# Three modulation edits at the start of a two-layer diffusion trunk: two blocks loaded first, blocks in pairs, two on VectorE

## The chip, the core and the metric

The kernel runs on one core of a Trainium2 chip. The metric is the device time of one execution in microseconds (us). Names of engines: PE is TensorE's matrix engine (PEld its weight loads), DVE is VectorE, ACT is ScalarE, POOL is GpSimd, and SP (SyncE) is the queue from which nearly all loads are issued.

## The reference

A trunk of two layers over 512 latent tokens and 256 context tokens, model width 2048, all in float32. What matters here is the start of a layer: a modulation vector is computed from the conditioning, and the normalized input is scaled and shifted by it before the input projection.

```python
shift, scale, gate = jnp.split(jax.nn.silu(c) @ ada_w + ada_b, 3, axis=-1)
shift_c, scale_c, gate_c = jnp.split(jax.nn.silu(c_ctx) @ ada_w + ada_b, 3, axis=-1)
h = rms_norm(x, norm_w) * (1.0 + scale[:, None]) + shift[:, None]
hc = rms_norm(xc, norm_w) * (1.0 + scale_c) + shift_c
(a_u, a_v, a_z, b_q, ...) = split_columns(h @ w_in)
...
y = jnp.concatenate([y_a, y_b, y_c], axis=-1) @ w_out
x_new = x + gate[:, None] * y
```

`ada_w` is 2048 x 6144 for each layer (50 MB). Behind the projection stand three branches (a gated MLP, a recurrent scan, differential attention) and an output projection; the change does not touch them.

## The kernel before, in words

The input lies transposed in memory: 16 tiles of 128 channels (`kt` 0 to 15) by 768 tokens. The columns of `ada_w` are cut into 24 blocks of 256 for each layer, 2 MB each: blocks 0 to 7 give the shift, 8 to 15 the scale (with the factor `gmul`), 16 to 23 the gate. Block b of the shift and block 8 + b of the scale together serve the tiles kt = 2b and 2b + 1.

A block is computed in one of two ways. `ada_pe` fetches it in five tiles of 128 x 768 and one of 128 x 256 (16 slices of the 2048 rows, three to a tile), multiplies each slice on PE with the conditioning (`sc`, 32 columns wide), copies the sum out of PSUM on VectorE (L271), folds it with two small matmuls against `sel` (in the pack of small constants) and ends in `ada_finish` (L221 adds the bias, L226 makes `gmul`). The tiles are taken in turn from 12 buffers (`ada_slot`): four named K and eight named adaw, which later hold the activations of kt 12 to 15; for the last blocks K, A and B. `ada_dve` fetches a block in eight tiles of 128 x 512 (two slices each, two buffers named adas) and multiplies and adds each slice on VectorE, two instructions a slice (L286 for the first, L288 for the rest), then transposes and reduces (L294, L296); `ada_close` folds it on PE. It is a generator that yields after each slice, so that other code can move it on by steps. In the kernel before, `ada_dve` is used for blocks 16 to 23 of layer 0 and all of layer 1, as a filler behind the lead stage.

Layer 0 begins so: the 16 tiles of x are loaded, ScalarE squares them and VectorE adds the squares up (L161); `rstd_broadcast` turns the sum into a factor for each token and spreads it over the partitions (`WT`). Then comes the lead stage in `run_layer`: four projections (`pp` and `a` in PSUM) run side by side over kt. For each kt, `h_tile` makes the modulated tile as a high part (`hi`, ScalarE L325) and a low part (`lo`, VectorE L326) of a product (`T`, VectorE L322), and PE adds three products (hi x wh, lo x wh, hi x wl) to each of the four projections, in pieces of 512 and 256 tokens. The weights come in groups of four kt: four tiles of 256 KB (`raw`), each split into `wh` (L332) and `wl` (L333). Ahead of each kt, `pre(kt + AHEAD)` with `AHEAD = 2` issues one modulation block, shift and scale by turns. After kt 15 the token groups (`TokGroup`) begin.

Who goes first: loads stay in program order on the SP queue, at most eight under way; a load that has to wait for its buffer holds up all loads behind it. On the other engines a scheduler orders the instructions when the program is built, and each engine then works through its own list strictly in order.

Of the kernel before, what the change touches and what calls it, by code (L numbers as in the profile page):

```python
# [11 lines left out]
F32 = mybir.dt.float32  # L12
# [9 lines left out]
P = 128  # L22
D = 2048
KT = D // P
# [19 lines left out]
def view(t, offset, dims):  # L44
    return bass.AP(t.tensor, t.offset + offset, [list(t.ap[0])] + [list(d) for d in dims])
# [3 lines left out]
def trunk(  # L49
# [10 lines left out]
    gp = ctx.enter_context(tc.tile_pool(name="gp", bufs=1))  # L60
# [23 lines left out]
    def load(dst, src):  # L84
        i = nc.sync.dma_start(dst, src)
        if pinned[0]:
            tc.keep_in_program_order(i)


    def nm(s):  # L90
        uid[0] += 1
        return f"{s}_{uid[0]}"

    BUFS = dict(A6=2, B6=2, C6=2, K3=4, Q3=4, T3=4, WT=2)
# [4 lines left out]
    def g3(tag, dt=F32, shape=(P, T)):  # L99
        return gp.tile(list(shape), dt, tag=tag, bufs=BUFS[tag], name=nm(tag))  # L100

    def small(tag, shape, dt=F32, bufs=3):
        return sp.tile(list(shape), dt, tag=tag, bufs=bufs, name=nm(tag))
# [4 lines left out]
    def p_one(shape):  # L108
        return ps.tile(list(shape), F32, tag="a1", bufs=4, name=nm("a1"))
# [38 lines left out]
    def xslot(i):  # L148
        if 8 <= i < 12:
            return g3("Q3")  # L150
        if i % 2 == 0:
            xslots.append(g6("A6" if i < 4 else "B6" if i < 8 else "C6"))
        return xslots[-1][:, i % 2, :]

    def square_into(acc, src, a, b, first, eng):
        if first:
            S.activation(acc[:, a:b], src[:, a:b], AF.Square)
            return
        sq = g3("T3")
        S.activation(sq[:, a:b], src[:, a:b], AF.Square)  # L160
        eng.tensor_tensor(acc[:, a:b], acc[:, a:b], sq[:, a:b], op=ALU.add)  # L161
# [58 lines left out]
    def ada_finish(l, n0, nn, pt):  # L220
        V.tensor_tensor(  # L221
            adaT[l][:, n0 : n0 + nn, :], pt, view(adab_s[l], n0, [[1, nn], [0, 2]]), op=ALU.add
        )
        if KT <= n0 < 2 * KT:
            k0 = n0 - KT
            V.scalar_tensor_tensor(  # L226
                gmul[l][:, k0 : k0 + nn, :],
                adaT[l][:, n0 : n0 + nn, :],
                1.0,
                view(normw_s[l], k0, [[1, nn], [0, 2]]),  # L230
                op0=ALU.add,
                op1=ALU.mult,
            )

    def ada_src(l, nb, kt, n):
        return ada_w[l, nb, :, kt : kt + n, :]
# [3 lines left out]
    def ada_slot(n0):  # L240
        tags = ["K3"] * 4
        if n0 < 12:
            tags = tags + [f"{w}{i}" for i in range(12, 16) for w in ("hi", "lo")]
        else:
            tags = tags + ["A6", "A6", "B6", "B6"]
        slots[0] += 1
        tag = tags[slots[0] % len(tags)]
        if tag in BUFS:
            return g3(tag, shape=(P, 3, 256))
        return ap.tile([P, 3, 256], F32, tag=tag, bufs=1, name=nm("adaw"))  # L250

    def ada_pe(l, n0):
        pa = p_one([P, 260])
        kt = 0
        while kt < KT:
            nk = min(3, KT - kt)
            wt = ada_slot(n0 % KT)
            load(wt[:, :nk, :], ada_src(l, n0 // 2, kt, nk))
            for k in range(nk):
                j = (kt + k) % 4  # L260
                PE.matmul(
                    pa[32 * j : 32 * j + 32, :256],
                    sc[:, kt + k, :],
                    wt[:, k, :],
                    start=(kt + k < 4),
                    stop=(kt + k >= KT - 4),
                    tile_position=(0, 32 * j),
                )
            kt += nk
        sb = g3("T3", shape=(P, 256))  # L270
        V.tensor_copy(sb, pa[:, :256])  # L271
        pt = pa[:, 256:260].rearrange("p (n i) -> p n i", i=2)
        for n in range(2):
            PE.matmul(pt[:, n, :], sb[:, n * P : (n + 1) * P], sel_s, start=True, stop=True)
        ada_finish(l, n0, 2, pt)

    def ada_dve(l, nb):
        acc = gp.tile([P, 2, 256], F32, tag="acc", bufs=1, name=nm("acc"))
        for kt in range(KT):
            if kt % 2 == 0:  # L280
                wt = wp.tile([P, 2, 256], F32, tag="adas", bufs=2, name=nm("adas"))
                load(wt, ada_src(l, nb, kt, 2))
            for i in range(2):
                sca = cc_s[:, kt, i : i + 1]
                if kt == 0:
                    V.tensor_scalar(acc[:, i, :], wt[:, 0, :], sca, None, op0=ALU.mult)  # L286
                else:
                    V.scalar_tensor_tensor(  # L288
                        acc[:, i, :], wt[:, kt % 2, :], sca, acc[:, i, :], op0=ALU.mult, op1=ALU.add
                    )  # L290
            yield

        tr = g3("T3", shape=(P, 16, 32))
        V.transpose(tr.rearrange("p a b -> p (a b)"), acc.rearrange("p a b -> p (a b)"))  # L294
        red = small("red", [P, T // 32], bufs=2)
        V.tensor_reduce(red[:, :16], tr, axis=AX.X, op=ALU.add)  # L296
        return red

    def ada_close(l, nb, red):
        pt = p_one([P, 2, 2])  # L300
        for q in range(4):
            PE.matmul(
                pt[32 * q : 32 * q + 32, :, :],
                fold,
                view(red, q, [[4, 2], [8, 2]]),
                start=True,
                stop=True,
                tile_position=(0, 32 * q),
            )
        ada_finish(l, 2 * nb, 2, pt)  # L310
# [111 lines left out]
    def prepare():  # L422
        nonlocal mask_s
        mask_s = const("mask", [P, MASKS * 32], U8)
        V.tensor_copy(mask_s, parts["masks"])
# [500 lines left out]
    AHEAD = 2  # L926
# [7 lines left out]
    TOKLAST = 4  # L934
    TOKFILL = (2, 2, 2, 3)
    LEVEL = 4
    LATE = 6
    TAILK = 2
    PREP = 16
# [2 lines left out]
    def advance(fill, n):  # L942
        for _ in range(n):
            if next(fill, 0) == 0:
                break

    def run_layer(l, xs, rb, pre, fillers, chain=None, ahead=()):
# [62 lines left out]
        for i in range(4):  # L1010
            pt = TokGroup(NCH if i < 3 else L.nch)
            for _ in pt.mm(nxt, acts):
                at += 1
                if at % LEVEL == 0:
                    next(lv, None)
# [95 lines left out]
        else:  # L1111
            for m in last:
                load(xscr[m], xs2[m])
            return xs2, rb, chain, ahead

    load(pk, pack)
    xs = []
    acc = g3("WT")
    for kt in range(KT):
        x = xslot(kt)  # L1120
        load(x, xT[kt])
        square_into(acc, x, 0, T, kt == 0, V)
        xs.append(x)
    def pre0(i):
        if i < KT:
            ada_pe(0, KT * (i % 2) + i - i % 2)
        if i == PREP:
            prepare()

    pre0(0)  # L1130
    rb = g3("WT")
    for _ in rstd_broadcast(acc, rb, 0, T):
        pass
    for i in range(1, AHEAD):
        pre0(i)

    def fill():
        late = None
        for l, b0 in ((0, 16), (1, 0)):
            for b in range(b0, 24):  # L1140
                steps = ada_dve(l, b)
                for _ in range(LATE):
                    next(steps)
                    yield
                if late is not None:
                    ada_close(*late)
                late = (l, b, (yield from steps))
        ada_close(*late)

    xs, rb, chain, ahead = run_layer(0, xs, rb, pre0, fill())  # L1150
    run_layer(1, xs, rb, lambda g: None, iter(()), chain, ahead)

# [85 lines left out]
```

## Time and profile before

| what | value |
|---|---|
| three timed runs, us | 2852.78, 2847.98, 2848.84 (median 2848.84) |
| profiled execution, us | 2852.29 |
| its span, us | 2850.2 |
| PE busy over the span | 2754.7 us, 97% |
| DVE, ACT, POOL busy | 55%, 34%, 11% |
| granted TensorE clock, mean | 0.99 of full speed |
| lead stage (first lead matmul to first token matmul) | 45.64 to 166.46 us |

The profiled execution is one run; its own time is its span and some 2 us around it. Busy time of an engine says nothing by itself: what counts is which wait ends last in the stage that is changed.

### The profile page before, as it was taken

The numbers are of one execution on the slowest core, as the hardware profiler recorded it, in microseconds if no ns is written. First come the engines' busy times: TensorE is split into PE (matmuls) and PEld (weight loads), VectorE is DVE, ScalarE is ACT, GpSimd is POOL, SyncE is SP. The second block draws the span as 40 slices with busy tenths as digits, with TensorE's granted clock in tenths as the row PEclk, the third lists the DMA queues.
The fourth block names the chain that finished last, engine by engine and source line by source line (L and its number), as shares of the span: only waits on it lengthen the run. The fifth ranks groups of instructions, "written<-read, shape, count | busy, mean of one in ns | idle before, by whom it ended". The sixth has DMA issues, their size and how long they took to land.

```text
span 2850.2 us, 44886 instructions
## 1 busy us (share of the span) xinstructions
PE 2754.7 (97%) x17524; PEld 2335.7 (82%) x17524; DVE 1566.4 (55%) x3224; ACT 966.2 (34%) x1852; POOL 324.1 (11%) x307
## 2 busy tenths in 40 slices
PE   5998999999999999999999999999999999999997
PEld 3676788888888888888888878888888888888786
DVE  4448867467687776766574272122444555554534
ACT  3222212323344434432311242223333544554321
POOL 0011000332000000001011011000342000000222
PEclk9999999999999999999999999999999999999998
DMA  9825555334343333435553222223232232234533
GB/s 347 276 93 175 177 158 158 85 104 133 95 119 101 108 105 98 122 93 171 177 146 105 80 77 87 89 89 96 75 86 73 74 85 60 82 93 125 166 97 94
DMA packets 184499, 340.24 MB, mean 119 GB/s; under 512 B 19296, under 2 KB 37856, under 8 KB 184288
## 3 DMA queue, kind: packets, MB, share of 16 engines
q1 hardware_dynamic: 177664, 325.33, 38.6%
q10 hardware_dynamic: 6624, 12.06, 1.1%
q8 instruction: 137, 2.24, 0.3%
q14 instruction: 74, 0.61, 0.1%
HBM read 306.91 MB, written 30.41 MB: 118 GB/s over the span
## 4 chain that ended last, share of the span: by engine, by line
PE 84%; DMA 6%; DVE 5%; issue 3%; POOL 1%; ACT 1%; SPq 0%; DVEq 0%; POOLq 0%; ACTq 0%
PE pp L78 68%; PE a L78 14%; DMA adas<-in_ada_w_dram 3%; DVE acc L288 2%; PE a L82 2%; DVE wl L333 1%; DMA adaw<-in_ada_w_dram 1%; POOL A L618 1%; POOL A L620 0%; DMA T<-y 0%; DMA raw<-in_w_in_dram 0%; DMA A<-in_ada_w_dram 0%; DMA B<-in_xT_dram 0%; DMA C<-in_xT_dram 0%; DVE C L616 0%
## 5 line engine op out<-in xcount | busy, mean ns | idle before, releaser
L78 PE MATMUL pp<-hi,wh 128*128 128x512 f32 (+1 forms) x3248 | 1134.3, 351 | 11.0 <-ACT hi L332 4.8
L78 PE MATMUL pp<-lo,wh 128*128 128x512 f32 (+1 forms) x3248 | 1136.6, 350 | 1.6 <-DVE lo L326 1.1
L78 PE MATMUL pp<-hi,wl 128*128 128x512 f32 (+1 forms) x3248 | 1130.9, 349 | 0.0
L333 DVE TENSOR_TENSOR wl<-raw,wh 128x512 fp32r<-128x512 f32 x634 | 448.3, 709 | 659.5 <-ACT wh L332 623.9
L332 ACT CAST wh<-raw 128x512 fp32r<-128x512 f32 x634 | 392.6, 621 | 1189.1 <-PE pp L78 1004.9
L78 PEld LDWEIGHTS pp<-hi,wh 128*128 128x128 f32 x3248 | 614.4, 190 | 94.6 <-ACT hi L332 5.3
L78 PEld LDWEIGHTS pp<-lo,wh 128*128 128x128 f32 x3248 | 616.1, 190 | 85.1 <-issue 6.7
L78 PEld LDWEIGHTS pp<-hi,wl 128*128 128x128 f32 x3248 | 615.0, 189 | 76.1 <-issue 0.2
L288 DVE SCALAR_TENSOR_TENSOR acc<-adas,cc_s,acc 128x256 f32<-128x256 f32 x960 | 421.5, 490 | 89.2 <-DMA adas<-in_ada_w_dram 87.8
L78 PE MATMUL pp<-wh,hi 128*128 128x512 f32 x512 | 200.7, 392 | 0.8 <-DVE WT L501 0.8
L78 PE MATMUL pp<-wl,hi 128*128 128x512 f32 x512 | 199.8, 390 | 0.0
L78 PE MATMUL pp<-wh,lo 128*128 128x512 f32 x512 | 199.5, 390 | 0.0
L830 POOL TENSOR_TENSOR ars<-e,mhalf 128x1 f32<-128x1 f32 x40 | 25.2, 630 | 962.8 <-DVE e L828 962.8
L78 PEld LDWEIGHTS pp<-wh,hi 128*128 128x128 f32 x512 | 96.5, 189 | 21.4 <-issue 1.2
L78 PEld LDWEIGHTS pp<-wh,lo 128*128 128x128 f32 x512 | 96.4, 188 | 20.3
L78 PEld LDWEIGHTS pp<-wl,hi 128*128 128x128 f32 x512 | 96.6, 189 | 19.9
L78 PE MATMUL a<-K,Q 128*128 128x512 f32 (+2 forms) x592 | 108.0, 321 | 0.9 <-DVE adaT L221 0.8
L793 ACT ACTIVATE C<-a,nb 128x256 f32<-128x256 f32 (+1 forms) x144 | 80.6, 567 | 57.5 <-DVE nb L789 54.7
L78 PEld LDWEIGHTS a<-K,Q 128*128 128x128 f32 x592 | 87.7, 190 | 10.5 <-DVE adaT L221 1.3
L78 PE MATMUL a<-wh,hi 128*128 128x512 f32 x224 | 90.7, 405 | 0.0
L78 PE MATMUL a<-wl,hi 128*128 128x512 f32 x224 | 88.3, 394 | 1.5 <-DVE wl L333 1.5
L78 PE MATMUL a<-wh,lo 128*128 128x512 f32 x224 | 88.3, 394 | 0.0
(220 smaller groups left out, 2526.2 us busy)
## 6 DMA issues: line engine op xcount, KB each, us to landing
raw<-in_w_in_dram SPq DMA_DIRECT2D x384, 256.0 KB, 3.1
adas<-in_ada_w_dram SPq DMA_DIRECT2D x256, 256.0 KB, 2.9
raw<-in_w_tok_dram SPq DMA_DIRECT2D x128, 256.0 KB, 2.7
raw<-in_w_out_dram SPq DMA_DIRECT2D x128, 256.0 KB, 3.1
adaw<-in_ada_w_dram SPq DMA_DIRECT2D x42, 384.0 KB, 7.2
t<-T ACTq DMA_DIRECT2D x46, 256.0 KB, 2.6
K<-in_ada_w_dram SPq DMA_DIRECT2D x28, 384.0 KB, 7.3
A<-t SPq DMA_DIRECT2D x11, 768.0 KB, 5.2
```

The costliest lines, as they stand in the source:

```text
L78: return PE.kept(nc.tensor.matmul(*args, **kw))
L82: return PE.kept(nc.tensor.transpose(*args, **kw))
L288: V.scalar_tensor_tensor(acc[:, i, :], wt[:, kt % 2, :], sca, acc[:, i, :], op0=ALU.mult, op1=ALU.add)
L332: S.copy(hi, src)
L333: V.tensor_tensor(lo, src, hi.bitcast(F32), op=ALU.subtract)
L618: G.tensor_tensor(kf, kf, view(tot, stride + 1, [[2, J], [0, m]]), op=ALU.mult)
L793: S.activation(pr[:, m, lo:hi], pt[:, : hi - lo], AF.Exp, bias=nb, scale=SCALE, accum_out=sums[:, m, i : i + 1] if len(parts) == 2 else sm ...
L830: G.tensor_tensor(rs, e0, mhalf[:, 0:1], op=ALU.pow)
```

## The change

Three edits, all in layer 0's start. `first_ada(0)` and `first_ada(1)` (block 0 for the shift and block 8 for the scale) stand ahead of the loads of x. In `pre0`, blocks are issued in pairs at every second kt instead of one at each kt. Blocks 7 and 15, which serve kt 14 and 15, are no longer computed by PE: `side_ada` computes them one after the other with `ada_dve`, moved on by `SIDE = 3` slices at each kt; its running sum takes one of the four buffers named T.

```diff
-    def ada_dve(l, nb):
-        acc = gp.tile([P, 2, 256], F32, tag="acc", bufs=1, name=nm("acc"))
+    def ada_dve(l, nb, tag="acc"):
+        acc = g3(tag, shape=(P, 2, 256)) if tag in BUFS else gp.tile([P, 2, 256], F32, tag=tag, bufs=1, name=nm(tag))
...
+    SIDE = 3
...
+    def first_ada(i):
+        ada_pe(0, KT * (i % 2) + i - i % 2)
+
+    def side_ada():
+        for nb in (KT // 2 - 1, KT - 1):
+            red = yield from ada_dve(0, nb, "T3")
+            ada_close(0, nb, red)
+
     load(pk, pack)
+    first_ada(0)
+    first_ada(1)
     xs = []
     acc = g3("WT")
     for kt in range(KT):
...
+    side = side_ada()
+
     def pre0(i):
-        if i < KT:
-            ada_pe(0, KT * (i % 2) + i - i % 2)
+        if i % 2 == 0 and i < KT - 2:
+            first_ada(i)
+            first_ada(i + 1)
+        if i < KT - 2:
+            advance(side, SIDE)
+        else:
+            advance(side, 1000)
         if i == PREP:
             prepare()
 
-    pre0(0)
     rb = g3("WT")
     for _ in rstd_broadcast(acc, rb, 0, T):
         pass
-    for i in range(1, AHEAD):
-        pre0(i)
```

The load queue (SP) behind the first group of weight tiles, before: the two constant tables `rope`, and then the tiles of the next blocks, one after the other.

```order
L85 DMA raw_334<-in_w_in_dram 128x512
L85 DMA rope_c<-in_rope_dram 128x512
L85 DMA rope_s<-in_rope_dram 128x512
L85 DMA K_70_341<-in_ada_w_dram 128x768
L85 DMA K_71_346<-in_ada_w_dram 128x768
L85 DMA K_72_351<-in_ada_w_dram 128x768
```

The same queue of the changed kernel, from the last tile of the pair for kt 2 and 3 to the first tiles of the pair for kt 4 and 5.

```order
L85 DMA K_83_400<-in_ada_w_dram 128x256
L85 DMA adas_410<-in_ada_w_dram 128x512
L85 DMA adas_416<-in_ada_w_dram 128x512
L85 DMA rope_c<-in_rope_dram 128x512
L85 DMA rope_s<-in_rope_dram 128x512
L85 DMA adas_455<-in_ada_w_dram 128x512
L85 DMA K_96_495<-in_ada_w_dram 128x768
L85 DMA K_97_500<-in_ada_w_dram 128x768
```

Three tiles of a side block now stand between one pair and the next. The third, adas_455, takes the buffer of adas_410, and the pair's tiles stand behind it.

VectorE's list from the copy of a finished block to the low part of kt 2, before (a_91 is a block's sum in PSUM).

```order
L271 COPY T_98_504<-a_91_475 128x256
L226 SCALAR_TENSOR_TENSOR gmul_96<-adaT_94,pack 128x4
L322 SCALAR_TENSOR_TENSOR T_101_511<-A_5_156,gmul_96,WT_255 128x512
L322 SCALAR_TENSOR_TENSOR T_101_511<-A_5_156,gmul_96,WT_255 128x256
L326 SCALAR_TENSOR_TENSOR lo_100_510<-T_101_511,adaT_94,hi_99_509 128x512
```

The same place in the changed kernel (a_95 and a_103 are the pair of blocks for kt 4 and 5, which the list has ahead of kt 2).

```order
L271 COPY T_102_523<-a_95_494 128x256
L288 SCALAR_TENSOR_TENSOR T_85_409<-adas_563,cc_s,T_85_409 128x256 x4
L221 TENSOR_TENSOR adaT_94<-a_95_494,pack 128x4
L271 COPY T_110_557<-a_103_528 128x256
L322 SCALAR_TENSOR_TENSOR T_115_575<-A_21_225,gmul_96,WT_290 128x512
L322 SCALAR_TENSOR_TENSOR T_115_575<-A_21_225,gmul_96,WT_290 128x256
L322 SCALAR_TENSOR_TENSOR T_119_616<-A_21_225,gmul_96,WT_290 128x512
L288 SCALAR_TENSOR_TENSOR T_85_409<-adas_569,cc_s,T_85_409 128x256
L322 SCALAR_TENSOR_TENSOR T_119_616<-A_21_225,gmul_96,WT_290 128x256
L288 SCALAR_TENSOR_TENSOR T_85_409<-adas_569,cc_s,T_85_409 128x256
L221 TENSOR_TENSOR adaT_94<-a_103_528,pack 128x4
L326 SCALAR_TENSOR_TENSOR lo_114_574<-T_115_575,adaT_94,hi_113_573 128x512
```

The products of kt 2 and 3 now stand behind both copies of the pair and behind four adds of a side tile, and the low part of kt 2 behind those of kt 3.

PE's list at kt 1, before: parts of a block (sc) stand between the lead projections.

```order
L78 MATMUL a_56_315<-hi_88_442,wl_337 128x512
L78 MATMUL a_102_542<-adaw_543,sc 32x256 x3
L78 MATMUL pp_312<-lo_89_443,wh_318 128x256
L78 MATMUL pp_312<-hi_88_442,wl_319 128x256
L78 MATMUL pp_313<-lo_89_443,wh_324 128x256
```

In the changed kernel the last projections of kt 1 are followed by the whole pair, tile after tile.

```order
L78 MATMUL pp_313<-hi_92_461,wh_336 128x256
L78 MATMUL pp_313<-lo_93_462,wh_336 128x256
L78 MATMUL pp_313<-hi_92_461,wl_337 128x256
L78 MATMUL a_95_494<-K_96_495,sc 32x256 x3
L78 MATMUL a_95_494<-K_97_500,sc 32x256 x3
L78 MATMUL a_95_494<-K_98_505,sc 32x256 x3
L78 MATMUL a_95_494<-adaw_510,sc 32x256 x3
```

No projection matmul stands between the tiles of a pair any more; those of kt 2 follow when the pair is through.

## Rows read from the trace of the kernel before

**Rows 1.** The page's first line.

```profile
span 2850.2 us, 44886 instructions
```

**Rows 2.** Windows: start:end, length, busy us by engine, PEclk, DMA share, GB/s.

```profile
45.60:166.00 120.40, 115.23 (x849) 78.88 (x850) 52.84 (x113) 28.77 (x52) 0.00 (x0) 0.99 0.75 255
...
76.00:84.00 8.00, 8.00 (x64) 4.75 (x64) 6.16 (x13) 3.29 (x7) 0.00 (x0) 1.00 1.03 403
...
148.00:152.00 4.00, 2.68 (x17) 1.89 (x16) 2.46 (x7) 1.12 (x2) 0.00 (x0) 1.00 0.24 70
152.00:156.00 4.00, 3.44 (x12) 2.48 (x10) 4.00 (x9) 2.24 (x4) 0.00 (x0) 0.68 0.00 0
```

**Rows 3.** PE's timeline: start, duration; kt 0, kt 10, first token matmul.

```profile
45.64 0.74 PE L78 MATMUL pp<-hi,wh 128*128 128x512 f32 x2 [0.81 <-ACT hi L325]
...
125.88 0.73 PE L78 MATMUL pp<-hi,wh 128*128 128x512 f32 x2
...
166.46 0.40 PE L78 MATMUL a<-wh,hi 128*128 128x512 f32 x1
```

**Rows 4.** PE's timeline: neighbouring projection matmuls of 512 and 256 columns.

```profile
159.69 0.39 PE L78 MATMUL pp<-lo,wh 128*128 128x512 f32 x1
...
160.15 0.28 PE L78 MATMUL pp<-hi,wh 128*128 128x256 f32 x1
...
160.74 0.28 PE L78 MATMUL pp<-hi,wl 128*128 128x256 f32 x1
```

**Rows 5.** The chain that ended last, 45 to 170 us.

```profile
67.08 3.45 PE a L78 x50
...
125.77 8.17 DMA A<-in_ada_w_dram
```

**Rows 6.** ScalarE's timeline: first and fourth weight tile of the first group.

```profile
32.65 0.62 ACT L332 CAST wh<-raw 128x512 fp32r<-128x512 f32 x1 [10.30 <-DMA raw<-in_w_in_dram]
...
36.49 0.62 ACT L332 CAST wh<-raw 128x512 fp32r<-128x512 f32 x1 [0.21 <-DMA raw<-in_w_in_dram]
```

**Rows 7.** Timeline: weight loads of PE that waited for modulation tiles.

```profile
24.40 0.19 PEld L78 LDWEIGHTS a<-K,sc 128*32 128x32 f32 x6 [0.78 <-DMA K<-in_ada_w_dram]
...
26.39 0.52 PEld L78 LDWEIGHTS a<-adaw,sc 128*32 128x32 f32 x8 [0.80 <-DMA adaw<-in_ada_w_dram]
```

**Rows 8.** The tile adas, 190 to 640 us: ns min/median/max; landing in us.

```profile
L288 DVE SCALAR_TENSOR_TENSOR acc<-adas,cc_s,acc x421: 435/479/1901, 198.5 to 639.7; 128x256 f32<-128x256 f32 x141
L85 SPq DMA_DIRECT2D adas<-in_ada_w_dram x114: 327/328/436, 194.8 to 599.4; - x114
L286 DVE TENSOR_SCALAR acc<-adas,cc_s x30: 336/345/928, 197.9 to 638.8; 128x256 f32<-128x256 f32 x30
...
DMA to landing us min/median/max: 2.5/2.9/5.0
```

**Rows 9.** Timeline, 14 to 46 us: from the squares' sum to kt 0.

```profile
14.00 10.52 DVE L161 TENSOR_TENSOR WT<-WT,T 128x768 f32<-128x768 f32 x10
...
27.93 0.97 DVE L171 STREAM_TRANSPOSE T<-WT 128x768 f32<-128x768 f32 x1
...
28.93 0.95 DVE L173 TENSOR_REDUCE red<-T 128x24 f32<-128x768 f32 x1
...
33.30 0.69 DVE L333 TENSOR_TENSOR wl<-raw,wh 128x512 fp32r<-128x512 f32 x1 [0.40 <-ACT wh L332]
...
37.01 0.37 ACT L201 COPY WT<-a 128x256 f32<-128x256 f32 x1
...
43.75 0.42 DVE L271 COPY T<-a 128x256 f32<-128x256 f32 x1 [1.38 <-PE a L78]
44.09 1.14 DVE L322 SCALAR_TENSOR_TENSOR T<-A,gmul,WT 128x512 f32<-128x512 f32 x2
...
44.87 1.12 ACT L325 ACTIVATE hi<-T,adaT 128x512 fp32r<-128x512 f32 x2 [7.49 <-DVE T L322]
...
45.62 1.15 DVE L326 SCALAR_TENSOR_TENSOR lo<-T,adaT,hi 128x512 fp32r<-128x512 f32 x2 [0.32 <-ACT hi L325]
```

**Rows 10.** The load queue's waits, 60 to 165 us: for what, us, times, longest.

```profile
SPq L85 <- PE a L78: 36.2, 26, 5.2
```

## The prediction

> **What bounds the kernel now.** The profiled execution spans 2850.2 us [rows 1] and took 2852.29 us; the three timed runs have a median of 2848.84, so what I work out on the span is carried over as a difference and set on the median. Over the whole span the matrix engine is busy 97%, so the first thing to read is where it is not: I went from the page's slices to the windows of the beginning, because all edits lie there.
>
> I call the lead stage the time from the first lead matmul (45.64 us) to the first matmul of the token group (166.46) [rows 3]. In it PE is busy 115 of 120 us and the DMA engines three quarters of the time [rows 2]. The reader should see that both are nearly full, in a stage where each of the 16 input tiles (kt 0 to 15) needs 4.2 us of projection matmuls and one 2 MB modulation block. The 4.2 comes from the spacing of neighbours, 0.23 us for 512 columns (159.69 to 160.15, halved) and 0.118 for 256 (160.15 to 160.74, over five) [rows 4], times 12 of each. A block's 16 matmuls cost about 2.2 us when its tiles have landed: 50 records in 3.45 us, two records to a matmul [rows 5]. The start of kt 0 is at 45.64 and that of kt 10 at 125.88 [rows 3]: 80.2 us for five pairs of tiles, 16.05 a pair; the last six tiles and their last blocks take 40.6.
>
> The loads are all on one queue in program order. Its longest waits in this stage are for PE, 36.2 us in 26 waits [rows 10]: a modulation tile can be fetched only when PE has emptied an older one of the 12 buffers. While transfers flow they move at 403 GB/s [rows 2], and two tiles of 384 KB land 0.99 us apart (26.39 minus 24.40, halved) [rows 7]. A pair of blocks is 10 such tiles and two thirds of one: **10.6 us**. The four 256 KB weight tiles of a group land slower, 1.28 us each (36.49 minus 32.65, over three) [rows 6]: **5.1 us** a group.
>
> **The change, part by part.**
>
> *Blocks 0 and 8 ahead of the input.* The queue up to the first weight tile carries the same bytes in another order, so that tile still lands at about 32.6 and the fourth at 36.4 [rows 6]. The input's last tile lands some 10.6 us later than before. The squares' sums ended at 24.5; they now start about 9 us later and end near 33. Then three weight splits (0.69 each) stand among the transposition and the reduction (0.97 and 0.95), which end near 37.3. From there to the broadcast factor it took 7.5 us before (29.88 to 37.38) [rows 9], so 44.8. Two blocks of PE work now lie in a time when PE has nothing else.
>
> *Pairs, and the end of the interleaving.* The next pair's tiles follow the weight tiles and land by 36.4 + 10.6 = 47.0, later than the broadcast. In the new PE order the pair stands as one burst ahead of the projection matmuls, and in VectorE's order kt 0's multiply stands behind the copies of both blocks. So kt 0 starts after the burst (47.3), a copy (0.42), two multiplies of the side block (0.34 each, 0.7), the tile's multiply (0.78 to ScalarE's start) and ScalarE's add (0.77 to PE's start) [rows 3, 8, 9]: **50.0**, 4.4 us later than before.
>
> *The side blocks (7 and 15) on VectorE.* Their 64 instructions are cheap: 0.48 us each [rows 8], 31 us, and VectorE is busy 53 of the stage's 120 [rows 2]. Their loads are not. There are two side buffers. In each round the third side tile has to wait until VectorE has done with the round's first one, and the last of those reads stands behind the burst, in most rounds behind the copies that follow it. The queue is in order, so all 12 tiles of the next pair (and every other round the four weight tiles) stand behind that third tile. Before, the queue ran ahead as buffers came free; now it stands still once a pair, from the landing of the second side tile until VectorE has come round. A side tile that meets an empty queue landed 2.9 us after issue (2.5 to 5.0) [rows 8].
>
> So from the issue I of a third side tile to the end of the next burst it takes 2.9 + 10.6 + 0.3 (the last matmul) = 13.8 us, or 18.9 where weights come between. From the burst to the next I I follow VectorE's new order with the durations of [rows 8, 9]: a side tile lands 0.4 after the burst (two thirds of 0.99 behind the pair's last tile), 0.48 a side instruction, 0.42 a copy, 1.14 a tile's multiply, 1.15 a tile's low part.
> - First round: burst 47.3; copy, two side multiplies, two tile multiplies (2.28), two side adds: I = 51.9.
> - Burst 65.7; four side adds stand ahead of the second copy: I = 68.0; kt 2 starts at 70.0.
> - Burst 86.9 (weights); two adds, copy, one tile, two adds: I = 90.8.
> - Burst 104.6; two adds, copy, two tiles, two adds: I = 109.6.
> - Burst 128.5 (weights); copy, two tiles, two adds, the low parts with two more adds: I = 135.7.
> - Burst 149.5; four adds, a weight split (0.69), a transposition (0.65, two thirds of the 0.97), multiply and add: kt 10 starts at **154.7**.
>
> PE's own work on a pair (8.4 us, some 2 more until the low part is there) ends before the next tiles have landed (60 against 65 in the first round), so it costs nothing there; without that cover it would.
>
> *The end.* The last six tiles have no block among them: 6 x 4.2 = 25.1, and 2.5 us in which kt 10's first four matmuls are done and VectorE has three more tiles ahead of the low part. The stage ends at 182.3 against 166.46: **15.8 us later**. Per part: +4.4 for kt 0, five pairs at 20.9 instead of 16.05 (+24.5), and 27.6 instead of 40.6 for the rest (-13.0). What comes behind is the same in order but for a few swaps, and waits for this stage; I cost it at nothing. On the median: 2848.8 + 15.8 = 2864.6, **2865**.
>
> **Bounds of the terms.** Landing on an empty queue 2.5 to 5.0: -2 to +10.5 in five rounds. I take 2.9, the median of 114 such loads. Weight tiles at the big tiles' rate (0.67 each) instead of 1.28: -4.9 in two rounds. The new order's waits on VectorE read wrong by half a microsecond: 2.5 either way. So this case holds +8 to +28, 2857 to 2877.
>
> For the same load the page "DMA: Bandwidth & Descriptors" of the Trainium skill (Anatomy of one DMA) gives about 2.0 us fixed plus the bytes at 436 GB/s, by my estimate 2.6 for 256 KB; the sum would be 1.5 us less, and the row decides.
>
> After 148 to 152 us, in which PE worked 2.7 of 4, the granted clock was 0.68 in the next 4 us [rows 2], partly the lower level of 1.2 GHz: 1.3 us lost. Each new pair starts after such a gap. Five of six starts lie under the wait for tiles; the last does not, so this adds at most 1.3, inside the range. The page "TensorE: Matmul & The Clock Gate" of the Trainium skill (HAM oscillation) says that waiting for DMA between bursts sends the engine back to half speed each time; it speaks against the change, and by it alone six starts would cost 8.
>
> **The rivals.**
> - *The loads do not stand still* (faster). If the third side tile found its buffer free, a round would last as long as its bytes: 10.6 + 3 x 0.66 + half of 5.1, 15.1. kt 10 at 125.6, the stage's end at 153: -13, 2836. For it: the queue's 36 us of waits for PE [rows 10] are what pairs and an early start could remove. Against it: the reader of the first tile stands behind the burst, and PE's own round is longer than 15.1 (next rival). It decides where the mean round falls under 17.8 us ((166.46 - 27.6 - 50.0) / 5).
> - *PE's round binds* (no change). 8.4 of projections, 4.4 for two blocks, 0.6 for their closing, a copy, multiply and add of 1.9 and 2 until the low part: 17.3; 50.0 + 86.5 + 27.6 = 164, -2, 2847. It needs the queue to be up to 3.6 us quicker a round than I read.
> - *Refilling is dearer* (slower still). The chain shows a tile issued at 125.77 that took 8.17 us [rows 5]. At that price five rounds add 26: 2891. That tile had four weight tiles ahead of it, so I give this little.
>
> **How the numbers follow.** Forecast 0.70, loads that don't pause 0.11, PE's round 0.11, dear refill 0.08. A measurement can tell 0.2%, 5.7 us. The first rival and a little of the second are faster (0.12), the rest of the second is the same (0.11), forecast and last rival are slower (0.77). The range leaves out the first and last rival, 0.19: 2846 to 2879.
>
> **What would show it.** In the changed kernel's trace: kt 0's first matmul near 50, kt 10's near 155, the first token matmul near 182; the load queue waiting for VectorE's side adds, several microseconds in each round (before, it hardly waited for VectorE but for weights); DMA share under 0.75 between 50 and 150; PE waiting for modulation tiles in each round. Wrong would be a trace in which the queue waits only for PE, or rounds under 17.8 us, or a later stage that takes back what the lead stage loses.

## The result, and the profile after

The changed kernel takes 2876.6 us (median of four runs, 2874.7 to 2879.5), the kernel before 2848.5 beside it, so the medians are 28 us apart. The estimated ratio is 1.0085 (95% interval 1.0069 to 1.0102), which is 24 us (20 to 29). The forecast was 2865, with 2879 as its upper end. The profiled execution took 2879.45 us.

The page's first line, against [rows 1]:

```profile
span 2877.4 us, 44842 instructions
```

PE's timeline at the three marks of [rows 3], the start of kt 0, of kt 10, and the first matmul of the token group:

```profile
51.19 0.73 PE L78 MATMUL pp<-hi,wh 128*128 128x512 f32 x2 [1.33 <-ACT hi L325]
...
165.55 1.23 PE L78 MATMUL pp<-hi,wh 128*128 128x512 f32 x2 [4.11 <-ACT hi L325]
...
194.59 0.40 PE L78 MATMUL a<-wh,hi 128*128 128x512 f32 x1
```

The lead stage ends 28.1 us later than before (194.59 against 166.46), the span is 27.2 longer: the loss lies in this stage alone, and nothing behind it adds to it or takes it back. kt 0 starts 5.5 us later, the five pairs from kt 0 to kt 10 take 114.4 us instead of 80.2 (22.9 a pair, before 16.05), the rest takes 29.0 instead of 40.6.

Windows of the stage and of one round (start:end, length, busy us of each engine, PEclk, DMA share, GB/s), against [rows 2]:

```profile
51.20:194.60 143.40, 118.86 (x761) 85.13 (x762) 77.03 (x176) 29.17 (x52) 0.00 (x0) 0.86 0.62 209
94.00:96.00 2.00, 1.60 (x6) 1.42 (x7) 2.00 (x6) 1.12 (x2) 0.00 (x0) 0.50 0.00 0
96.00:98.00 2.00, 2.00 (x6) 1.61 (x5) 2.00 (x6) 0.00 (x0) 0.00 (x0) 0.50 0.54 160
98.00:100.00 2.00, 2.00 (x7) 1.61 (x7) 1.97 (x6) 0.00 (x0) 0.00 (x0) 0.50 0.89 292
100.00:102.00 2.00, 2.00 (x15) 1.83 (x14) 2.00 (x5) 1.12 (x2) 0.00 (x0) 0.89 1.02 359
102.00:104.00 2.00, 2.00 (x34) 1.21 (x36) 1.44 (x4) 0.00 (x0) 0.00 (x0) 1.00 0.99 378
104.00:106.00 2.00, 2.00 (x19) 1.37 (x12) 0.00 (x0) 0.00 (x0) 0.00 (x0) 1.00 1.03 394
106.00:108.00 2.00, 2.00 (x11) 1.16 (x10) 0.00 (x0) 0.00 (x0) 0.00 (x0) 1.00 1.03 416
```

Read the last column of the small windows downwards. From 94 to 96 us no byte moves from memory, in a stage that before had its DMA engines busy three quarters of the time on average. Then the rate climbs, and it takes ten microseconds to be back at what [rows 2] show in full flow. The clock column shows 0.50 in the same place: PE has waited and starts the pair at the lower of its two levels.

What the load queue waited for between 40 and 185 us (for what, us, times, longest; lines left out), against [rows 10]:

```profile
SPq L85 <- DMA adas<-in_ada_w_dram: 26.5, 5, 6.5
...
SPq L85 <- DVE adaT L221: 13.3, 4, 4.3
...
SPq L85 <- DVE gmul L226: 6.4, 1, 6.4
...
SPq L85 <- PE a L78: 4.5, 4, 3.4
```

In the kernel before, over the same window:

```profile
SPq L85 <- PE a L78: 42.0, 33, 5.2
```

Before, this queue waited for PE. Now it waits for the landing of side tiles, then for VectorE, and hardly for PE. (The lines with `adaT` and `gmul` name instructions that VectorE's list has next to the side adds; the buffer that is waited for is a side tile's. Among the lines left out is a wait for weight splits, 16.6 us, of which 14.3 are one wait behind the last block.) One stop in full, from the queue's timeline and its waits between 62.8 and 71.1 us:

```profile
61.94 9.44 SPq L85 DMA_DIRECT2D adas<-in_ada_w_dram  x3
71.43 1.85 SPq L85 DMA_DIRECT2D raw<-in_w_in_dram  x4
```

```profile
SPq L85 <- DMA adas<-in_ada_w_dram: 6.5, 1, 6.5
SPq L85 <- DVE adaT L221: 1.8, 1, 1.8
```

Three side tiles stand in one row; two are issued at once, the third only at 71.05, and the weight tiles and the next pair stand behind it. The 8.3 us between have two parts: the round's first side tile has to land, and it was issued behind all the pair's tiles, so it comes last (6.5); then VectorE has to read it (1.8). When the third tile may go, every load issued before has landed. That is how the queue runs dry.

### The profile page after: what moved, and what is told of

Same layout as the page of the kernel before. It is cut to its first block, busy times and chain, and to the rows that moved or that the text cites. A ratio compares the mean times of both kernels' runs of the same rounds, so it can differ in the third digit from the quotient of the medians.

```text
span 2877.4 us, 44842 instructions
## 1 busy us (share of the span) xinstructions
PE 2765.2 (96%) x17468; PEld 2348.2 (82%) x17468; DVE 1592.2 (55%) x3290; ACT 965.9 (34%) x1852; POOL 325.0 (11%) x307
## 4 chain that ended last, share of the span: by engine, by line
PE 79%; DVE 7%; DMA 6%; issue 4%; POOL 2%; ACT 1%; SPq 1%; DVEq 0%; POOLq 0%; ACTq 0%
PE pp L78 65%; PE a L78 13%; DMA adas<-in_ada_w_dram 4%; DVE acc L288 3%; PE a L82 2%; DMA adaw<-in_ada_w_dram 1%; DVE wl L333 1%; POOL A L618 1%; POOL A L620 1%; SPq L85 1%; DVE WT L161 0%; DVE T L322 0%; DMA T<-y 0%; DMA K<-in_ada_w_dram 0%; DVE C L616 0%
## 5 line engine op out<-in xcount | busy, mean ns | idle before, releaser
L78 PEld LDWEIGHTS pp<-hi,wh 128*128 128x128 f32 x3248 | 619.0, 191 | 97.2 <-ACT hi L325 10.7
L288 DVE SCALAR_TENSOR_TENSOR acc<-adas,cc_s,acc 128x256 f32<-128x256 f32 x960 | 421.9, 491 | 87.3 <-DMA adas<-in_ada_w_dram 86.1
L78 PEld LDWEIGHTS pp<-wh,hi 128*128 128x128 f32 x512 | 96.9, 189 | 21.5 <-issue 1.2
```

The source lines that it names most:

```text
L78: return PE.kept(nc.tensor.matmul(*args, **kw))
L288: V.scalar_tensor_tensor(acc[:, i, :], wt[:, kt % 2, :], sca, acc[:, i, :], op0=ALU.mult, op1=ALU.add)
```

## The experiments

Theory: the third side tile of a round, with two buffers, stops the one in-order queue until VectorE has come round. Rivals: the pairs, the early blocks, the side blocks' work as such, or PE's clock cost the time. Beside the experiments the kernel before took 2853 to 2854 us, 5 more than beside the change; each ratio is to the runs of before on the same chip, and the stage's marks are compared with one another. Marks are the first lead matmul (kt 0) and the first token matmul (end), in us.

| kernel | kt 0 | end | ratio, 95% interval |
|---|---|---|---|
| before | 45.64 | 166.46 | 1 |
| the change | 51.19 | 194.59 | 1.0085 (1.0069 to 1.0102) |
| e1 change, third side tile in a buffer of its own | 50.66 | 163.74 | 0.9977 (0.9968 to 0.9987) |
| e2 change, side tiles on GpSimd's queue | 54.10 | 178.91 | 1.0020 (1.0011 to 1.0030) |
| e3 change without side blocks | 49.89 | 161.99 | 0.9987 (0.9975 to 0.9998) |
| e4 change without pairs | 48.95 | 170.10 | 1.0002 (0.9993 to 1.0012) |
| e5 change, two side tiles a round | 50.64 | 166.92 | 0.9991 (0.9978 to 1.0003) |
| e6 change, pairs of half the bytes | 49.03 | 160.48 | 0.9984 (0.9973 to 0.9996) |
| e7 change, more matmuls in the bursts | 54.78 | 202.60 | 1.0128 (1.0106 to 1.0150) |
| e8 before, pairs alone | 51.81 | 163.27 | 0.9980 (0.9969 to 0.9991) |
| e9 before, side blocks alone | 45.45 | 169.81 | 0.9999 (0.9990 to 1.0009) |
| e10 before, early blocks alone | 48.68 | 169.66 | 0.9998 (0.9989 to 1.0008) |
| e11 e1 without pairs | 50.02 | 162.68 | 0.9971 (0.9959 to 0.9983) |

The differences in time (by the ratios) and in the stage's end agree within 4.5 us, but for e2 (7); the marks come from one execution each.

**e1: a buffer for the third tile.** The buffer is one of the weight tiles' five (`raw`); none is added.

```diff
-wt = wp.tile([P, 2, 256], F32, tag="adas", bufs=2, ...)
+third = tag != "acc" and side_n[0] % 3 == 2
+side_n[0] += 1
+if third:
+    wt = wp.tile([P, 2, 256], F32, tag="raw", bufs=5, ...)
+else:
+    wt = wp.tile([P, 2, 256], F32, tag="adas", bufs=2, ...)
```

> The third side tile of each round gets a buffer of the weight tiles' pool, so that it does not wait for the reads of the round's first side tile; nothing else is edited. Theory (the third side tile holds up everything behind it on the in-order queue until VectorE has come round): the queue no longer stands still between the second side tile and the next pair, a round falls from 22.9 us to 16 to 19, kt 10's first lead matmul comes at 131 to 146 instead of 165.6, the stage ends at 160 to 175 instead of 194.6, and the time is 2842 to 2858. Rival (the pairs' order and the later start cost the time, the side tiles' wait stands beside them): rounds stay above 21, the time above 2868.

The queue's waits between 40 and 170 us, and PE's timeline at kt 2, kt 10 and the end:

```profile
SPq L85 <- PE a L78: 21.5, 21, 6.0
...
SPq L85 <- DVE adaT L221: 2.0, 1, 2.0
SPq L85 <- DMA adas<-in_ada_w_dram: 2.0, 7, 0.7
```

```profile
67.70 0.73 PE L78 MATMUL pp<-hi,wh 128*128 128x512 f32 x2 [0.81 <-ACT hi L332]
...
136.47 1.12 PE L78 MATMUL pp<-hi,wh 128*128 128x512 f32 x2 [1.40 <-ACT hi L332]
...
163.74 0.40 PE L78 MATMUL a<-wh,hi 128*128 128x512 f32 x1
```

This takes 31 us out of the stage. Same blocks, same pairs, same bytes, same arithmetic; the waits for side tiles fall from 26.5 us to 2.0, those under `adaT` from 13.3 to 2.0, those for PE rise from 4.5 to 21.5, and a round takes (136.47 - 50.66) / 5 = 17.2 us. The kernel is now faster than before. The theory stands; a rival that keeps the loss elsewhere would have had to show it here.

**e2: another queue.**

```diff
+    def side_load(dst, src):
+        nc.gpsimd.dma_start(dst, src)
...
-                load(wt, ada_src(l, nb, kt, 2))
+                (load if tag == "acc" else side_load)(wt, ada_src(l, nb, kt, 2))
```

> The side tiles are issued from GpSimd's queue; buffers and order on the engines that compute stay. The third side tile then still waits for VectorE, but the next pair's tiles do not stand behind it. Theory (order of one queue): as with a buffer of its own, rounds of 16 to 19 us, the stage's end at 160 to 175, the time 2842 to 2858; SP's waits for VectorE's side adds (26 us between 40 and 185) are gone. Rival A (the side blocks' bytes or VectorE's work on them cost the time, not the order of the queue): over 2868. Rival B (a second queue that waits disturbs the first one's transfers): between the two, with transfers of the pair's tiles slower than the 0.99 us of a tile of 384 KB.

The expectation was missed: 178.91, between the two. Of the 28.1 us that the stage lost, 15.7 are gone, and with them the load queue's waits for side adds. Three pieces of the chain at one of the places where time is still lost (start, us, what):

```profile
83.85 6.80 issue
...
90.67 7.06 DMA adas<-in_ada_w_dram
...
97.82 1.68 DVE T L291 x4
```

The timelines of GpSimd, of ScalarE (the next weight tile) and of PE at kt 5:

```profile
90.67 0.56 POOL L91 DMA_DIRECT2D adas<-in_ada_w_dram  x1 [6.82 <-DVE gmul L229]
```

```profile
96.03 0.62 ACT L335 CAST wh<-raw 128x512 fp32r<-128x512 f32 x1 [7.80 <-DMA raw<-in_w_in_dram]
```

```profile
102.26 1.22 PE L78 MATMUL pp<-hi,wh 128*128 128x512 f32 x2 [8.28 <-ACT hi L328]
```

What the chain calls issue is GpSimd's queue, which waits 6.82 us until VectorE has come round to the buffer. A side tile issued so late still takes 7.06 us to land; VectorE works through its list in order, so kt 5's multiply stands behind the four side instructions that want this tile, and PE idles 8.28 us ahead of kt 5. But the side tile is not alone there: ahead of the four stands the split of a weight tile that landed only at 96.0, and VectorE idled 4.78 us for this split and then 0.45 for the side tile. So a second queue takes the wait for side adds off the load queue; of the 12.5 us by which the stage is still longer than before, how much is the side tiles' was not separated. That the second queue slowed the transfers themselves (rival B) was not shown.

**e3: no side blocks; e8: pairs alone; e10: early blocks alone; e9: side blocks alone; e4: no pairs.** The parts of the change, left out or by themselves. From the changed kernel, e3 hands blocks 7 and 15 back to PE:

```diff
-        if i % 2 == 0 and i < KT - 2:
+        if i % 2 == 0 and i < KT:
             first_ada(i)
             first_ada(i + 1)
-        if i < KT - 2:
-            advance(side, SIDE)
-        else:
-            advance(side, 1000)
```

and e4 issues each block ahead of its own tile:

```diff
-        if i % 2 == 0 and i < KT - 2:
-            first_ada(i)
-            first_ada(i + 1)
         if i < KT - 2:
+            first_ada(i)
             advance(side, SIDE)
```

From the kernel before, e8 only pairs the blocks:

```diff
-        if i < KT:
-            ada_pe(0, KT * (i % 2) + i - i % 2)
+        if i % 2 == 0 and i < KT:
+            ada_pe(0, i)
+            ada_pe(0, KT + i)
```

e9 only gives blocks 7 and 15 to VectorE (`side_ada` as in the change):

```diff
-        if i < KT:
+        if i < KT - 2:
             ada_pe(0, KT * (i % 2) + i - i % 2)
+        if 2 <= i < KT - 2:
+            advance(side, SIDE)
+        elif i >= KT - 2:
+            advance(side, 1000)
```

and e10 only takes blocks 0 and 8 ahead of the loads of x:

```diff
+    ada_pe(0, 0)
+    ada_pe(0, KT)
...
-        if i < KT:
+        if 2 <= i < KT:
             ada_pe(0, KT * (i % 2) + i - i % 2)
```

> Blocks 7 and 15 go back to PE as a pair of their own; the two early blocks and the pairs stay. Theory: without side tiles the queue waits only for PE's buffers; the round is PE's own, 16 to 17.3 us, and kt 0 starts without the four side multiplies at 49 to 50.5; the last pair's block work comes back to PE (4.4 us). Stage end at 160 to 172, time 2842 to 2854. Rival (pairs and early start alone make the loss): 2865 or more.

> The blocks are taken one by one again, each ahead of its own tile kt; the early blocks and the side blocks stay, with the same two buffers. Theory: a side tile still waits for VectorE in the midst of the queue, but only one block stands behind it, and PE has the other tile's matmuls meanwhile; so the stall is partly covered: stage end at 170 to 182, time 2852 to 2864. Rival (it is only the side tiles' place in the queue, whatever the grouping): as after, 2870 to 2880. Other rival (the pairs alone cost it): 2846 to 2851.

> The kernel before with its blocks in pairs and nothing else: no early blocks, no side blocks. Theory (a pair's bytes are hidden as long as the queue may run ahead): rounds of PE's length, 16 to 17.2 us, no stop of the queue; the first round starts later by a pair's burst, kt 0 at 48 to 51; stage end 160 to 168, within 5 us of the kernel before either way. Rival (bursts make PE wait for tiles that were hidden between matmuls): stage end over 172, 6 us or more over the kernel before.

> The kernel before with the side blocks on VectorE alone: no early blocks, blocks one by one. Theory (third side tile in two buffers stops the queue wherever it stands): the queue waits for VectorE's side adds as in the run without pairs; stage end 168 to 174 against 166.5 of the kernel before, 2 to 8 us over it. Rival (side tiles only hurt together with pairs, whose bursts VectorE has to come round): no wait of the queue for the side adds, stage end under 166, at or under the kernel before.

> The kernel before with only the first two blocks ahead of the input. Theory: bytes are only moved in the queue, two blocks of PE work (4.4 us) go to a time when PE has nothing else, kt 0 starts 1 to 3 us later; stage end 162 to 167, within 5 us of the kernel before, rather under it. Rival (the later end of the input's squares puts kt 0 off and nothing makes up for it, as the prediction's +4.4): stage end 169 to 171, 3 to 5 us over.

The ends of the stage in PE's timeline, of e3, then e8, e9 and e10:

```profile
161.99 0.40 PE L78 MATMUL a<-wh,hi 128*128 128x512 f32 x1
```

```profile
163.27 0.40 PE L78 MATMUL a<-wh,hi 128*128 128x512 f32 x1
```

```profile
169.81 0.40 PE L78 MATMUL a<-wh,hi 128*128 128x512 f32 x1
```

```profile
48.68 0.73 PE L78 MATMUL pp<-hi,wh 128*128 128x512 f32 x2 [0.81 <-ACT hi L325]
...
169.66 0.40 PE L78 MATMUL a<-wh,hi 128*128 128x512 f32 x1
```

Pairs alone shorten the stage by 3.2 us, early blocks alone lengthen it by 3.2 (kt 0 starts 3.0 later, as the rival said, and nothing in the stage makes up for it), both together shorten it by 4.5. Side blocks alone lengthen it by 3.4, in line with the theory; with early blocks and without pairs by 3.6. The times of e9 and e10 show nothing of this (ratios 0.9999 and 0.9998): the 2 to 8 us over before that the theory gave for e9, and the 3 to 5 that the rival gave for e10, were missed. No part and neither of the two combinations costs more than 4 us, and all three together cost 28. The loss belongs to side blocks and pairs together, early blocks being there: the queue's waits for VectorE ahead of side tiles are there in e4 as well, 24.0 us in all (40 to 170 us; L288 are the side adds),

```profile
SPq L85 <- PE a L78: 15.3, 16, 4.4
SPq L85 <- DVE adaT L221: 15.2, 4, 6.2
SPq L85 <- DVE T L288: 8.8, 7, 2.9
```

but there one block stands behind the stop, not two, and PE has a tile's projections to go on with. Pairs with side blocks and without early ones were not run.

**e5: two side tiles a round.**

```diff
-SIDE = 3
+SIDE = 2
```

> One number is changed: the side block goes forward by two input rows a block instead of three, so a round has two side tiles and two buffers for them; the last two of the 16 side tiles come at the end, ahead of kt 14. Theory (it is the third tile in two buffers that stops the queue): each side tile finds its buffer free for a round, rounds fall from 22.9 us to about 17.2, as they did when the third tile had a buffer of its own, kt 10's first lead matmul at 136 to 140, stage end 164 to 170 (the two late tiles add 1 to 5 us). Time between 4 us under and 4 us over the kernel before. Rival (what the side tiles cost goes by their number): two thirds of the 5.7 us a round stay, rounds of 21, stage end near 184, 15 us or more over the kernel before.

PE's timeline at kt 10 and the end:

```profile
138.30 1.22 PE L78 MATMUL pp<-hi,wh 128*128 128x512 f32 x2 [0.40 <-ACT hi L325]
...
166.92 0.40 PE L78 MATMUL a<-wh,hi 128*128 128x512 f32 x1
```

Rounds of 17.5 us: one side tile less a round took off all but 0.4 us of what its own buffer took off in e1. All 16 side tiles are still loaded and worked off, the last ones at the end; from 50 to 120 us the queue waits only 1.6 us for side adds. What counts is the number of tiles in a round against the number of buffers.

**e6: the refill by itself.**

```diff
-def ada_pe(l, n0):
+def ada_pe(l, n0, kts=KT):
...
-    while kt < KT:
+    while kt < kts:
```

> Measures the refill by itself: the six pairs behind the early one load and multiply only the first 8 of their 16 input rows (half of those sums is left out), all else stays, so 2.1 MB less stand behind each third side tile. Read from the issue of a third side tile to the end of the next burst, in rounds without weight tiles (16.1 us in the changed kernel): theory (a fixed cost of some 5 us for setting an empty queue going again, over the bytes at 403 GB/s): 16.1 - 5.2 = 10.9, between 10.2 and 11.6. Rival (a lower rate throughout, 4.45 MB in 16.1 us): 2.36 MB take 8.5, under 9.5. The prediction's own terms would give 2.9 + 5.3 + 0.3 = 8.5 too. The time falls to 2845 to 2858 by the first, less by the second.

The queue's timeline in one round of e6, and the landing of its last tile (K):

```profile
82.67 0.33 SPq L85 DMA_DIRECT2D adas<-in_ada_w_dram  x1
83.09 2.28 SPq L85 DMA_DIRECT2D adaw<-in_ada_w_dram  x5
85.42 0.64 SPq L85 DMA_DIRECT2D K<-in_ada_w_dram  x1
```

```profile
DMA to landing us min/median/max: 6.2/6.2/6.2
```

The same of the changed kernel:

```profile
95.78 0.33 SPq L85 DMA_DIRECT2D adas<-in_ada_w_dram  x1
...
103.56 0.33 SPq L85 DMA_DIRECT2D K<-in_ada_w_dram  x1
```

```profile
DMA to landing us min/median/max: 7.6/7.6/7.6
```

In e6 PE is still at its projections when the tiles are there, so I read to the landing of the pair's last tile in both. Changed kernel: 103.56 + 7.6 - 95.78 = 15.4 us for 4.46 MB. e6: 85.42 + 6.2 - 82.67 = 9.0 for 2.36 MB. The fixed cost would have given 10.2, the low rate 8.2: neither. A line through the two gives 3.05 us a MB, 328 GB/s, and 1.8 us besides. So most of what the refill costs above the forecast goes with the bytes. Two points and one round each don't settle it finer.

**e7: the clock by itself.**

```diff
+if l == 0 and n0 not in (0, KT) and kt + k >= 4:
+    PE.matmul(pa[32 * j : 32 * j + 30, :256], sc[:, kt + k, 2:], wt[:, k, :],
+              start=False, stop=False, tile_position=(0, 32 * j))
 PE.matmul(pa[32 * j : 32 * j + 32, :256], sc[:, kt + k, :], ...
```

> The clock by itself: in the six later pairs 12 of a block's 16 matmuls are each preceded by one of the same size whose weights are zeros (it adds nothing to the sum), so that PE has some 0.7 us of work instead of 0.36 per landed tile. Theory (the loads bind, the clock costs only at kt 10's start): the first matmuls of each pair run at 0.23 us spacing instead of 0.43, rounds stay at 22.4 to 23.2, kt 10 to the first token matmul falls from 29.0 to about 27.7; time 1 to 4 us under the changed kernel's 2876, so 24 to 27 over the kernel before. Rival (the fall of the clock in six starts costs its 8 us): 8 or more under the changed kernel. A third way: the added matmuls don't lift the clock; then no change.

A miss: the stage became 8.0 us longer. PE's timeline at the burst ahead of kt 2, at kt 10 and at the end:

```profile
67.38 1.70 PE L78 MATMUL a<-K,sc 128*32 128x256 f32 x25
...
175.42 1.06 PE L78 MATMUL pp<-hi,wh 128*128 128x512 f32 x2 [1.40 <-ACT hi L334]
...
202.60 0.40 PE L78 MATMUL a<-wh,hi 128*128 128x512 f32 x1
```

A window of e7 from kt 10 on, with the granted clock in the third column from the end:

```profile
175.40:178.00 2.60, 2.58 (x13) 1.67 (x14) 2.60 (x8) 1.49 (x3) 0.00 (x0) 0.55 0.00 0
```

PE came to this burst at 67.38, straight from the projections, and found tiles there to be worked off in a row (25 records without a wait). There the 24 added matmuls (2.8 us at the 0.118 of [rows 4]) were on the path, not in a gap. kt 0, which has such a burst ahead of it too, starts 3.6 us later (54.78 against 51.19), and rounds are 1.3 longer ((175.42 - 54.78) / 5 = 24.1). From kt 10 to the end it took 27.2 us instead of 29.0, as expected, but not because the clock was kept up: it was 0.55 there, and e1 has 27.3 for this part without added matmuls, behind the same wait of 1.40 us. So the experiment does not price the clock.

The chain of the changed kernel bounds it. From 60 to 100 us:

```profile
by line: DMA adaw<-in_ada_w_dram 54.4%; DMA adas<-in_ada_w_dram 33.4%; SPq L85 15.7%; DVE T L288 6.9%; DVE T L322 4.3%; issue 3.8%; ACT hi L325 2.8%; DVE T L271 1.7%; DVE adaT L221 0.6%; DVEq L288 0.1%
```

No piece of it is PE's. From 51 to 142 us PE is on the chain for 0.97 us, with the last matmuls of a pair; only in the fifth round, from 142.1 to 154.7, does its own work bind. There the granted clock was 0.50 from 144 to 148 us, which costs some 2 us by my estimate (half of these four). That is little beside the 34 us by which five rounds were longer than before.

**e11: e1 without pairs.** The edits of e1 and e4 together.

> The third side tile with a buffer of its own, and blocks one by one instead of in pairs; early and side blocks as in the change. Theory (the stop of the queue is all that the side blocks cost, and PE saves their 4.4 us): the 8.8 us of waits of the queue for the side adds in the run without pairs are gone, stage end from 170.1 to 161 to 166, time 4 to 9 us under the kernel before, at or below the version with pairs. Rival (the loss of the run without pairs lies in the single blocks' order, not in the stop): stage end stays over 168, at or over the kernel before.

The queue's waits in e11, 40 to 170 us (L295 are the side adds):

```profile
SPq L85 <- PE a L78: 17.6, 19, 3.9
...
SPq L85 <- DVE T L295: 2.2, 2, 1.9
...
SPq L85 <- DVE adaT L221: 0.8, 1, 0.8
```

The stage ends at 162.68 and the time is 0.29% under before (interval 0.17 to 0.41), the lowest of all that were run; the waits for side adds fell from 8.8 us to 2.2, those under `adaT` from 15.2 to 0.8. With no stop in the queue, no gain of pairs can be told: the intervals of e1, e8 and e11 overlap.

## Why the prediction was right, and where it was short

**The mechanism was right.** "The queue is in order, so all 12 tiles of the next pair stand behind that third tile": e1 takes away nothing but this wait, e5 one side tile a round, and rounds fall from 22.9 to 17.2 and 17.5. Of the signs, the DMA share from 50 to 150 us is 0.70 (before, 0.84), PE waits for modulation tiles in four of the five rounds, and none of the three signs of being wrong came. That the wait ends partly with VectorE was right too, but the larger part of a stop (26.5 us of 46) is the landing of the round's first side tile behind the pair's last bytes. The prediction had this in the order of its sum (side tile lands 0.4 behind the burst), not in its words.

**The term that was mis-sized** is the refill behind a stop: "10.6 (12 tiles)" for the pair and 5.1 for weight tiles, both at the spacing of tiles in full flow. To the landing of the last tile the forecast was 13.5 us, and 18.6 with weight tiles. Measured: 15.9 and 15.4, and 20.9 and 21.1 with weights (last issues at 60.62, 103.56, 85.57, 130.62, third side tiles at 52.72, 95.78, 71.05, 116.09), and 15.4 in the fifth round, in which the queue also waited 4.3 us for PE. That is 1.9 to 2.5 a round, some 11 us in five, against 9.7 by which all five rounds were longer than forecast (114.4 against 104.7). What pays is whatever stands first behind the stop. With weight tiles ahead, these took 7.7 and 7.6 us from the landing of the third side tile (forecast 5.1), and the pair behind them 10.4 and 10.7, as forecast; without them the pair took 12.8 both times. The 403 GB/s were read where transfers flowed; behind an empty queue the rate is 160, 292, 359 and 378 GB/s in the first four windows with transfers, and the next round's two side tiles move among the pair's last ones.

The landing of 2.9 on an empty queue was not the fault: the third side tile landed after 3.1, 2.8, 2.6, 2.9 and 2.8 us. For this load the prediction also gave a figure from the page "DMA: Bandwidth & Descriptors" of the Trainium skill (Anatomy of one DMA). There it stands for loads issued from GpSimd, and these go by SyncE's queue.

That was the bound to set: "Landing on an empty queue 2.5 to 5.0" bounded the first tile and left the twelve behind it at full rate, and for weight tiles only the gain was bounded (-4.9). So it is luck that the time still lay inside the range, 2.4 us under its upper end: the room came from a landing that hardly varied, and the refill used it up. With the measured rounds in place of the forecast ones the sum is 50.0 + 114.4 + 27.6 = 192.0; the two smaller terms make it 194.6. In the prediction's own arithmetic two lines stand 0.2 and 0.3 us above their terms (I = 51.9 and 135.7), and the bounds add up to +6.4 to +28.8, not +8 to +28; that decides nothing here.

**Smaller terms.** kt 0 at 50.0: measured 51.2. Tail 27.6: 29.0, with PE at a granted clock of 0.50 from 165.5 to 172 us, behind a wait of 4.11 us at kt 10's start (in e1, after 1.40 us of wait, 27.3). This start was priced at 1.3 at most and costs 1.4 above the forecast. The granted clock is 0.50 from 94 to 100 us, behind a burst between waits for tiles. With this the trace agrees with the rule that the prediction cited from the page "TensorE: Matmul & The Clock Gate" of the Trainium skill (HAM oscillation), that such bursts bring half speed. That it costs 8 us over six starts no run here shows: the chain gives some 2 us in the fifth round and none in the four before it, and e1 starts kt 10 near half speed too (two matmuls in 1.12 us, in [rows 3] 0.73) and beats the kernel before. Later stages were costed at nothing, and the span agrees to 1 us.

**The rivals.** The rival that PE's round binds gave 17.3 us a round and an end at 164, if the queue were quicker: with the stop removed, e1 shows 17.2 and 163.74. It was not the case here, but it is the next bound below; in e1 PE's weight loads wait only 0.8 us for modulation tiles from 51 to 165 us. The rival with loads that don't stand still (15.1 a round) never showed, since PE's round lies above it. The dearer refill (2891) had the right place and the wrong price: 26 us over the forecast, of which some 11 came, by another mechanism than one late tile a round.

## What to carry to other kernels

Before a side stream goes into an in-order queue, count its tiles for a round against its buffers: one tile too many makes the whole queue wait for the slowest reader, and a buffer or a smaller step cured it here, where another queue took off little more than half. Price a stop as the stop and the refill: behind an empty queue the next tiles don't come at the rate of full flow. And parts that cost 3 us each can cost 28 together, so measure the combination, and repair the part that couples them.

## What the runs showed of the hardware

Not expected: after a pause of the only load queue the transfers took some 10 us to reach 400 GB/s again (0, 160, 292, 359, 378, 394, 416 GB/s in windows of 2 us from 94 to 108; at the first stop 15, 242, 346, 372, 400 from 52 to 62), though 13 issues were out within 8 us (95.78 to 103.56). A lone tile of 256 KB landed after 2.6 us in the same place, a tile of 128 KB issued as the last of them after 7.6. Whether the climb lies in the queue or in the memory was not tried.
